# Strassen's seven block products in 8 of 32 pairs of k tiles of each down-projection sweep

## The chip, the cores and the metric

One NeuronCore of one Trainium2 chip runs the whole program in one launch. The metric is device time in microseconds (us). The kernel before took 2149.73, 2150.02 and 2151.38 us in three runs, median 2150.02 us.

## The reference

A two-layer encoder trunk on one sequence of 256 tokens, width 2048, all in float32. Each layer has an attention sub-layer (layer 0 differential attention, layer 1 windowed grouped-query attention with a sink, both with four memory heads) and an MLP. What matters here is the MLP:

```python
h = rms_norm(x, norm_mlp[i])
x = x + jnp.square(jax.nn.relu(h @ w_up[i])) @ w_down[i]
```

Per layer `w_up` is 2048 x 8192 and `w_down` 8192 x 2048, so the down projection multiplies 256 x 8192 by 8192 x 2048: 64 k tiles of 128 rows.

## The kernel before

**Splitting.** Every float32 operand of a large product is split into a part `hi` rounded to fp32r (ScalarE, a cast) and a rest `lo` (VectorE, `raw - hi`). A product is then three fp32r matmuls: hi x hi, hi x lo, lo x hi. Weights arrive as pieces of 128 x 1024 floats, 512 KB each. `fetch` (L171) issues the load on SyncE's queue into one of 4 `raw` buffers, and the split into one of 4 `hi` and 4 `lo` buffers. `piece` (L188) keeps two pieces ahead of the one in use; a list `plan` (L156 to L166) gives the order of all pieces.

**The MLP** (`mlp`, L647). The up projection leaves the hidden values feature-major in 16 tiles `hT`, the first six in the one large buffer `big` (which holds the attention bias table outside the MLP), the other ten in the pool `blk`. The down projection makes two sweeps per layer, one for each half of the 2048 output columns. A sweep holds four PSUM banks (`ps[n][t]`: two chunks of 512 columns by two tiles of 128 tokens; pool `mm` in the first sweep, `aux` in the second) and steps through 32 pairs of k tiles. A pair takes two weight pieces, one for each chunk, and two splits of hidden tiles (`h2_of`, into the pool `h2`), and issues 2 k tiles x 2 token tiles x 2 chunks x 3 = 24 matmuls of 128 x 128 by 128 x 512. A layer ends with `finish`, which adds the banks to the residual `xt`. In the last sweep of the program the last two pairs are held back, so that bank after bank can be finished and sent out.

**Order.** The engines run their instructions in order; a scheduler settles the order on each engine when the kernel is built, and can move a split ahead where its buffers are free. With 4 `hi` and 4 `lo` buffers, the split of the next pair starts when TensorE has ended the pair before the present one. The bias table of layer 1 is loaded back into `big` (`bias_load`, L579) in the second sweep of layer 0, once the hidden tiles in `big` have been read.

A pair's matmuls are these:

```python
for kk in range(2):
    for t in range(2):
        for n in range(2):
            mms(n, t, 2 * j + kk, *w2[n], x2[kk])
```

Of the kernel before, what the change touches and what calls it, by code (L numbers as in the profile page):

```python
# [14 lines left out]
F32 = mybir.dt.float32  # L15
# [4 lines left out]
ALU = mybir.AluOpType  # L20
# [14 lines left out]
WARM = 16  # L35
LAM_INIT = 0.8 - 0.6 * math.exp(-0.3 * 0)
# [10 lines left out]
def trunk(ctx: ExitStack, tc: tile.TileContext, xin, xtok, memin, pos, rel, gcol, rows,  # L47
# [19 lines left out]
    def half(tag):  # L67
        return xp.tile([P, 2, 256], F32R, tag=tag, name=nm(tag), bufs=16 if tag == "x2" else 12)

    def blk(shape, dt):  # L70
        return xp.tile(shape, dt, tag="blk", name=nm("blk"), bufs=10)
# [86 lines left out]
    def plan_down(name):  # L158
        plan.extend((name, c, j) for h in range(2) for j in range(32) for c in (2 * h, 2 * h + 1))
# [47 lines left out]
    def make_x2(src, g, tag="x2"):  # L207
        t = half(tag)
        split_gain(t[:, 0, :], t[:, 1, :], src, g)
        return t  # L210
# [161 lines left out]
    def diff_head(hl, qT, kT, v, bias, H2, hg):  # L372
# [62 lines left out]
        def finish():  # L435
# [9 lines left out]
    def plain_head(hl, kl, qT, kT, v, bias, sink, H2, hg, tag):  # L445
# [42 lines left out]
        def finish():  # L488
# [9 lines left out]
            t = half(tag)  # L498
            split(t[:, 0, :], t[:, 1, :], o)
            H2[hg] = t  # L500
# [106 lines left out]
    def mem_part(layer, qm, qd, H2):  # L607
        M2 = [None] * KT
        box = {}

        def before(j):
# [15 lines left out]
        heads = [plain_head(h, h, qm, kT, vbox, None, None, H2, 12 + h, "x2") for h in range(4)]  # L627
# [8 lines left out]
    def out_proj(layer, H2):  # L636
        X2 = [None] * KT
# [9 lines left out]
    def mlp(layer, X2, last):  # L647
        hT = []
        wide = big([P, 6, 4, S])
        for c in range(16):  # L650
# [3 lines left out]
            ht = wide[:, c] if c < 6 else blk([P, 4, S], F32)  # L654
# [6 lines left out]
        N2 = [None] * KT  # L661

        def h2_of(k):
            t = half("h2")
            split(t[:, 0, :], t[:, 1, :], hT[k // 4][:, k % 4, :])
            return t


        for half_ in range(2):
# [4 lines left out]
            def mms(n, t, k, hi, lo, x2):  # L674
                ws = slice((k % 2) * 512, (k % 2) * 512 + 512)
                xh = x2[:, 0, t * P:(t + 1) * P]
                xl = x2[:, 1, t * P:(t + 1) * P]
                nc.tensor.matmul(ps[n][t], lhsT=xh, rhs=hi[:, ws], start=(k == 0), stop=False)  # L678
                nc.tensor.matmul(ps[n][t], lhsT=xh, rhs=lo[:, ws], start=False, stop=False)  # L679
                nc.tensor.matmul(ps[n][t], lhsT=xl, rhs=hi[:, ws], start=False, stop=(k == 4 * KT - 1))  # L680

            def finish(n, t):
                c = chunks[n]
                d = xt[:, t, c * 512:(c + 1) * 512]
                nc.vector.scalar_tensor_tensor(d, ps[n][t], r2[:, t:t + 1], d, op0=ALU.mult, op1=ALU.add)
# [164 lines left out]
```

## Time and profile before

| quantity | value |
|---|---|
| median of 3 runs | 2150.02 us |
| the profiled execution's own time | 2150.42 us |
| its span | 2148.6 us |
| TensorE busy | 2137.6 us (99%) |
| VectorE busy | 1315.6 us (61%) |
| ScalarE busy | 1083.6 us (50%) |
| mean DMA rate | 190 GB/s |
| granted TensorE clock | 1.00 |

The span runs from the first to the last instruction; the execution's own time is 1.8 us longer. Busy shares are means over stages with different limits. A matmul's duration is longer than the distance to the next one, since matmuls are pipelined: the distance between starts is the pace. The four down sweeps begin at about 784.8, 958.9, 1795.0 and 1969.5 us.

### The profile page before, as it was taken

Reading aid. Unit: us, or ns where it says so; the run is one execution under the profiler, and the core shown is the slowest. Engines: PE = TensorE matmul, PEld = TensorE weight load, DVE = VectorE, ACT = ScalarE, POOL = GpSimd, SP = SyncE. Lnnn points to the kernel's source line nnn. Section 1 sums busy time; section 2 is a strip of 40 time slices with the busy share of each in tenths; the row PEclk is TensorE's granted clock in tenths of the full one; section 3 lists DMA queues with packets and bytes.
Section 4 is the critical chain, followed back from the end, with each engine's and each line's share of the span. In section 5 each row is a group of like instructions: output and inputs, shape, how many; then the busy total and the mean of one; then the engine's idle time right before and its main releaser. Section 6 shows DMA issues by size and latency. Waiting matters only on the chain.

```text
span 2148.6 us, 29416 instructions
## 1 busy us (share of the span) xinstructions
PE 2137.6 (99%) x11116; PEld 1806.4 (84%) x11116; DVE 1315.6 (61%) x2067; ACT 1083.6 (50%) x1740; POOL 35.7 (2%) x61
## 2 busy tenths in 40 slices
PE   9999999999999999999999999999999999999999
PEld 7877878888888888888888888888888888888887
DVE  7667786565555555566556677655555556556554
ACT  6456675454444445555545566554444444544443
POOL 1200020000000000000000000000000000000000
PEclk9999999999999999999999999999999999999999
DMA  8865565666666666666656656566666666666654
GB/s 292 237 209 154 157 195 153 187 183 189 185 194 188 191 186 193 193 195 235 198 194 192 181 167 178 155 183 183 185 195 188 192 189 185 196 196 212 192 193 148
DMA packets 114959, 409.24 MB, mean 190 GB/s; under 512 B 13568, under 2 KB 14336, under 8 KB 114560
## 3 DMA queue, kind: packets, MB, share of 16 engines
q1 hardware_dynamic: 111840, 401.01, 60.9%
q0 software_dynamic: 1536, 4.20, 0.8%
q10 hardware_dynamic: 1440, 2.15, 0.3%
q8 instruction: 87, 1.43, 0.3%
q14 instruction: 56, 0.46, 0.1%
HBM read 401.93 MB, written 5.37 MB: 190 GB/s over the span
## 4 chain that ended last, share of the span: by engine, by line
PE 97%; DMA 1%; DVE 1%; ACT 1%; issue 0%; SPq 0%; POOL 0%; ACTq 0%; DVEq 0%; POOLq 0%
PE mm L289 11%; PE aux L289 11%; PE mm L276 9%; PE mm L277 9%; PE mm L278 9%; PE mm L293 6%; PE aux L293 6%; PE mm L680 5%; PE mm L679 5%; PE mm L678 5%; PE aux L679 5%; PE aux L680 5%; PE aux L678 5%; DMA raw<-in_w_a 1%; PE aux L368 1%; PE aux L339 1%
## 5 line engine op out<-in xcount | busy, mean ns | idle before, releaser
L185 DVE TENSOR_TENSOR lo<-raw,hi 128x1024 fp32r<-128x1024 f32 (+1 forms) x744 | 892.7, 1214 | 747.7 <-ACT hi L184 747.3
L184 ACT CAST hi<-raw 128x1024 fp32r<-128x1024 f32 (+1 forms) x744 | 764.3, 1044 | 815.2 <-PE aux L289 194.1
L276 PE MATMUL mm<-hi,x 128*128 128x512 f32 x704 | 281.3, 401 | 2.0 <-ACT hi L184 2.0
L277 PE MATMUL mm<-lo,x 128*128 128x512 f32 x704 | 276.3, 392 | 2.1 <-DVE lo L185 2.1
L278 PE MATMUL mm<-hi,x 128*128 128x512 f32 x704 | 275.9, 392 | 0.0
L289 PE MATMUL mm<-x,hi 128*128 128x512 f32 x1024 | 247.4, 391 | 0.0
L289 PE MATMUL aux<-x,hi 128*128 128x512 f32 x1024 | 246.9, 391 | 0.0
L289 PEld LDWEIGHTS mm<-x,hi 128*128 128x128 f32 x1024 | 188.2, 188 | 36.8 <-DVE xt L642 0.5
L289 PEld LDWEIGHTS aux<-x,hi 128*128 128x128 f32 x1024 | 188.2, 188 | 36.4
L679 PE MATMUL aux<-lo,h 128*128 128x512 f32 x512 | 199.5, 390 | 0.5 <-DVE lo L185 0.5
L680 PE MATMUL aux<-hi,h 128*128 128x512 f32 x512 | 199.2, 389 | 0.0
L678 PE MATMUL aux<-hi,h 128*128 128x512 f32 x512 | 199.2, 389 | 0.0
L678 PE MATMUL mm<-hi,h 128*128 128x512 f32 x512 | 199.2, 389 | 0.0
L679 PE MATMUL mm<-lo,h 128*128 128x512 f32 x512 | 199.2, 389 | 0.0
L680 PE MATMUL mm<-hi,h 128*128 128x512 f32 x512 | 199.2, 389 | 0.0
L276 PEld LDWEIGHTS mm<-hi,x 128*128 128x128 f32 x704 | 132.2, 188 | 29.1 <-ACT hi L184 3.3
L277 PEld LDWEIGHTS mm<-lo,x 128*128 128x128 f32 x704 | 132.6, 188 | 28.2 <-DVE lo L185 4.2
L278 PEld LDWEIGHTS mm<-hi,x 128*128 128x128 f32 x704 | 132.2, 188 | 27.9 <-DVE x L201 0.2
L293 PEld LDWEIGHTS mm<-x,lo 128*128 128x128 f32 x1024 | 131.4, 191 | 4.8
L293 PEld LDWEIGHTS aux<-x,lo 128*128 128x128 f32 x1024 | 131.3, 191 | 5.0
L293 PE MATMUL mm<-x,lo 128*128 128x256 f32 x1024 | 133.3, 283 | 0.0
L293 PE MATMUL aux<-x,lo 128*128 128x256 f32 x1024 | 132.8, 283 | 0.0
(166 smaller groups left out, 2114.8 us busy)
## 6 DMA issues: line engine op xcount, KB each, us to landing
raw<-in_w_up SPq DMA_DIRECT2D x256, 512.0 KB, 3.9
raw<-in_w_down SPq DMA_DIRECT2D x256, 512.0 KB, 4.2
raw<-in_w_a SPq DMA_DIRECT2D x72, 512.0 KB, 4.0
raw<-in_w_out SPq DMA_DIRECT2D x64, 512.0 KB, 3.6
raw<-in_w_b SPq DMA_DIRECT2D x48, 512.0 KB, 3.7
raw<-in_w_mem SPq DMA_DIRECT2D x32, 512.0 KB, 3.8
raw<-in_w_a SPq DMA_DIRECT2D x16, 256.0 KB, 5.7
blk<-bkt POOLq DMA_DIRECT2D x32, 128.0 KB, 8.8
```

The costliest lines, as they stand in the source:

```text
L184: nc.scalar.copy(hi[:, s], raw[:, s])
L185: nc.vector.tensor_tensor(lo[:, s], raw[:, s], as32(hi)[:, s], op=ALU.subtract)
L276: nc.tensor.matmul(ps[t], lhsT=xh, rhs=hi[:, ws], start=(k == 0), stop=False)
L277: nc.tensor.matmul(ps[t], lhsT=xh, rhs=lo[:, ws], start=False, stop=False)
L278: nc.tensor.matmul(ps[t], lhsT=xl, rhs=hi[:, ws], start=False, stop=(k == KT - 1))
L289: nc.tensor.matmul(ps[o], lhsT=hi[:, cols(k % 2, o)], rhs=x2.rearrange("p a s -> p (a s)"), start=(k == 0), stop=(k == 2 * nj - 1))
L293: nc.tensor.matmul(ps[o][:, 256:512], lhsT=lo[:, cols(k % 2, o)], rhs=x2[:, 0, :], start=False, stop=False)
L339: nc.tensor.transpose(out=pt[:, h * P:(h + 1) * P], in_=qn[t][:, h * P:(h + 1) * P], identity=ident)
L368: nc.tensor.transpose(out=pt[:, kt * S + qt * P:kt * S + (qt + 1) * P], in_=p_of(qt)[:, kt * P:(kt + 1) * P], identity=ident)
L678: nc.tensor.matmul(ps[n][t], lhsT=xh, rhs=hi[:, ws], start=(k == 0), stop=False)
L679: nc.tensor.matmul(ps[n][t], lhsT=xh, rhs=lo[:, ws], start=False, stop=False)
L680: nc.tensor.matmul(ps[n][t], lhsT=xl, rhs=hi[:, ws], start=False, stop=(k == 4 * KT - 1))
```

## The change

In each sweep the pairs 5, 8, 11, 14, 17, 20, 23 and 26 (`FAST`) are computed as a 2 x 2 by 2 x 2 block product with seven block products instead of eight (the Winograd form of Strassen's scheme): the blocks are token tile by k tile on one side, k tile by column chunk on the other. Three of the products go straight into three of the four banks. The other four go into four more banks (`side`, the pool of the other sweep), summed over the eight fast pairs, and are added to the residual by `add_side` after pair 26.

- Weights are laid out anew on the host (`_pairs`): a piece now holds two of the four blocks of a pair, [b00, b11] and [b10, b01]. Bytes and number of pieces are the same. An ordinary pair's matmuls pick their block from either piece.
- `fetch_sums` makes for a fast pair two 128 x 1024 tiles of block sums of weights on VectorE and splits them like a piece; of the second piece only the first half is still split.
- `seven` makes four 128 x 128 block sums of the hidden tiles (`v`) and splits them.
- The pools `x2` and `h2` now hand out tiles of two k tiles (8 and 6 of them, before 16 and 12 halves), so one split covers 512 columns. The hidden tiles in `big` are now chunks 4 to 9, before 0 to 5. With that the load of the bias table stands in SyncE's queue behind the weight loads of pair 18 of the sweep, before behind those of pair 9.

```diff
+FAST = (5, 8, 11, 14, 17, 20, 23, 26)
...
     def plan_down(name):
-        plan.extend((name, c, j) for h in range(2) for j in range(32) for c in (2 * h, 2 * h + 1))
+        plan.extend((name, h, j) for h in range(2) for j in range(64))
...
+    def fetch_sums(key, raw, hi, lo):
+
+        first = newest[0]
+        tag = "blk" if key[:2] == ("down0", 1) else "x2"
+        a, b = quad(tag, (P, 2, 512), F32), quad(tag, (P, 2, 512), F32)
+        nc.vector.tensor_tensor(a, first.rearrange("p (a n) -> p a n", a=2),
+                                raw[:, 512:1024].unsqueeze(1).broadcast_to([P, 2, 512]), op=ALU.add)
+        nc.vector.tensor_tensor(b[:, 0, :], a[:, 1, :], first[:, 0:512], op=ALU.add)
+        nc.vector.tensor_tensor(b[:, 1, :], b[:, 0, :], raw[:, 0:512], op=ALU.add)
+        split(hi[:, 0:512], lo[:, 0:512], raw[:, 0:512])
+        ah, al, bh, bl = [quad("x2", (P, 2, 512)) for _ in range(4)]
+        split(ah, al, a)
+        split(bh, bl, b)
+        sums[key] = (ah, al, bh, bl)
...
+        seven = name.startswith("down") and j % 2 == 1 and j // 2 in FAST
...
             behind[0] = nc.sync.dma_start(raw[:, s], src[:, s])
-            nc.scalar.copy(hi[:, s], raw[:, s])
-            nc.vector.tensor_tensor(lo[:, s], raw[:, s], as32(hi)[:, s], op=ALU.subtract)
+            if seven:
+                fetch_sums((name, c, j), raw, hi, lo)
+            else:
+                split(hi[:, s], lo[:, s], raw[:, s])
...
-            ht = wide[:, c] if c < 6 else blk([P, 4, S], F32)
+            ht = wide[:, c - 4] if 4 <= c < 10 else blk([P, 4, S], F32)
...
+            def seven(j, two, x2):
+
+                ah, al, bh, bl = [v.rearrange("p a n -> p (a n)") for v in sums.pop((f"down{layer}", half_, 2 * j + 1))]
+                t2 = quad("h2", (P, 2, 512))
+                v = t2k([P, 512])
+                h = hidden(j)
+                h4 = h.rearrange("p (a s) -> p a s", a=4)
+                nc.vector.tensor_tensor(v[:, 0:256].rearrange("p (a s) -> p a s", a=2), h4[:, 0:4:3, :],
+                                        h4[:, 1:2, :].broadcast_to([P, 2, P]), op=ALU.subtract)
+                nc.vector.tensor_tensor(v[:, 256:384], h[:, 384:512], v[:, 0:128], op=ALU.add)
+                nc.vector.tensor_tensor(v[:, 384:512], h[:, 256:384], v[:, 256:384], op=ALU.subtract)
+                split(t2[:, 0, :], t2[:, 1, :], v)
+                at = [slice(i * P, (i + 1) * P) for i in range(4)]
+                f, e = j == FAST[0], j == FAST[-1]
+                three(side[0], f, e, x2, at[0], two[0], lower)
+                three(ps[0][0], False, False, x2, at[2], two[1], lower)
+                three(ps[1][0], False, False, t2, at[3], two[0], upper)
+                three(side[1], f, e, t2, at[0], (ah, al), upper)
+                three(side[3], f, e, t2, at[1], (ah, al), lower)
+                three(side[2], f, e, t2, at[2], (bh, bl), lower)
+                three(ps[0][1], False, False, x2, at[3], (bh, bl), upper)
...
+            def add_side():
+
+                q1, u2, u3, u4, u5 = [t2k([P, 512]) for _ in range(5)]
+                nc.scalar.copy(q1, side[0])
+                nc.vector.tensor_tensor(u2, side[2], q1, op=ALU.subtract)
+                nc.vector.tensor_tensor(u4, side[1], u2, op=ALU.subtract)
+                nc.vector.tensor_tensor(u3, u2, side[3], op=ALU.subtract)
+                nc.vector.tensor_tensor(u5, u3, side[1], op=ALU.subtract)
+                add_to(0, 0, q1)
+                add_to(0, 1, u4)
+                add_to(1, 0, u3)
+                add_to(1, 1, u5)
...
             for j in range(32):
-                w2 = [piece(f"down{layer}", c, j) for c in chunks]
-                x2 = [h2_of(2 * j), h2_of(2 * j + 1)]
+                if j == FAST[0]:
+                    side = [bank("aux" if half_ == 0 else "mm") for _ in range(4)]
+                two = [piece(f"down{layer}", half_, 2 * j + i) for i in range(2)]
+                x2 = h2_of(j)
...
+                if j in FAST:
+                    seven(j, two, x2)
+                else:
+                    for kk in range(2):
+                        for t in range(2):
+                            for n in range(2):
+                                mms(n, t, 2 * j + kk, two, x2)
+                if j == FAST[-1]:
+                    add_side()
```

`three` issues the three matmuls of a block product (hi x hi, hi x lo, lo x hi). The scheduler's order around a fast pair follows, at two places.

On VectorE before, in the first sweep of layer 0: the splits of pairs 10 (raw_8193, raw_8199), 11 (raw_8235, raw_8241) and 12, with two hidden tiles between.

```order
L185 TENSOR_TENSOR lo_8195<-raw_8193,hi_8194 128x1024
L185 TENSOR_TENSOR lo_8201<-raw_8199,hi_8200 128x1024
L205 TENSOR_TENSOR h_8418<-blk_6218,h_8418 128x256
L205 TENSOR_TENSOR h_8457<-blk_6218,h_8457 128x256
L185 TENSOR_TENSOR lo_8237<-raw_8235,hi_8236 128x1024
L185 TENSOR_TENSOR lo_8243<-raw_8241,hi_8242 128x1024
L205 TENSOR_TENSOR h_8460<-blk_6218,h_8460 128x256
L205 TENSOR_TENSOR h_8499<-blk_6415,h_8499 128x256
```

Now the same stretch: the splits of pair 10 (raw_8168, raw_8174), hidden tiles of pairs 12 and 13, the sums a (x_8217) and b (x_8218) of the fast pair 11 (raw_8207, raw_8213), their rests al and bl, the split of pair 11 itself, a hidden tile, and the split of pair 12.

```order
L242 TENSOR_TENSOR lo_8170<-raw_8168,hi_8169 128x1024
L242 TENSOR_TENSOR lo_8176<-raw_8174,hi_8175 128x1024
L242 TENSOR_TENSOR h_8314<-big_4604,h_8314 128x512
L242 TENSOR_TENSOR h_8366<-big_4604,h_8366 128x512
L194 TENSOR_TENSOR x_8217<-raw_8207,raw_8213 128x1024
L196 TENSOR_TENSOR x_8218<-x_8217,raw_8207 128x512
L197 TENSOR_TENSOR x_8218<-x_8218,raw_8213 128x512
L242 TENSOR_TENSOR x_8225<-x_8217,x_8224 128x1024
L242 TENSOR_TENSOR x_8227<-x_8218,x_8226 128x1024
L242 TENSOR_TENSOR lo_8209<-raw_8207,hi_8208 128x1024
L242 TENSOR_TENSOR lo_8215<-raw_8213,hi_8214 128x512
L242 TENSOR_TENSOR h_8405<-big_4604,h_8405 128x512
```

Between the splits of pairs 10 and 11 there were two operations of 256 columns; now there are two of 512, and the five of the sums, which stand ahead of the rests of pair 11 itself.

On TensorE, the last matmul of pair 10 and the start of pair 11, before (hi_8236 and hi_8242 are the two pieces) and now.

```order
L680 MATMUL mm_7814<-hi_8200,h_8250 128x512
L678 MATMUL mm_7811<-hi_8236,h_8289 128x512
L679 MATMUL mm_7811<-lo_8237,h_8289 128x512
L680 MATMUL mm_7811<-hi_8236,h_8289 128x512
L678 MATMUL mm_7813<-hi_8242,h_8289 128x512
L679 MATMUL mm_7813<-lo_8243,h_8289 128x512
```

```order
L713 MATMUL mm_7778<-hi_8169,h_8232 128x512
L711 MATMUL aux_7987<-hi_8208,h_8271 128x512
L712 MATMUL aux_7987<-lo_8209,h_8271 128x512
L713 MATMUL aux_7987<-hi_8208,h_8271 128x512
L711 MATMUL mm_7775<-hi_8214,h_8271 128x512
L712 MATMUL mm_7775<-lo_8215,h_8271 128x512
L713 MATMUL mm_7775<-hi_8214,h_8271 128x512
L711 MATMUL mm_7777<-hi_8208,h_8274 128x512
L712 MATMUL mm_7777<-lo_8209,h_8274 128x512
L713 MATMUL mm_7777<-hi_8208,h_8274 128x512
L711 MATMUL aux_7988<-x_8224,h_8274 128x512
```

The second matmul of the pair still needs the rest of the first piece, and the fifth that of the second piece; the sums (x_8224) are first read by the tenth. TensorE has 96 matmuls fewer in the whole program.

## Rows read from the trace of the kernel before

**Rows 1.** Page, part 1: engine, busy us, share of span, instructions.

```profile
PE 2137.6 (99%) x11116; PEld 1806.4 (84%) x11116; DVE 1315.6 (61%) x2067; ACT 1083.6 (50%) x1740; POOL 35.7 (2%) x61
```

**Rows 2.** Three sweeps: us, PE, PEld, DVE, ACT, POOL busy, clock, DMA, GB/s.

```profile
784.80:958.90 174.10, 174.10 (x770) 144.16 (x769) 103.29 (x138) 87.30 (x133) 0.00 (x0) 1.00 0.61 192
958.90:1134.00 175.10, 174.59 (x777) 144.13 (x776) 100.60 (x127) 87.71 (x131) 3.06 (x2) 1.00 0.64 207
...
1969.50:2144.50 175.00, 175.00 (x773) 144.63 (x771) 97.30 (x121) 81.01 (x115) 0.00 (x0) 1.00 0.58 189
```

**Rows 3.** TensorE's waits in layer 0's sweeps: us, times, longest.

```profile
PE aux L679 <- DVE lo L185: 0.5, 1, 0.5
```

**Rows 4.** TensorE, timeline, 72 matmuls in a row: start, duration, work.

```profile
859.83 0.39 PE L678 MATMUL mm<-hi,h 128*128 128x512 f32 x1
...
875.92 0.39 PE L680 MATMUL mm<-hi,h 128*128 128x512 f32 x1
```

**Rows 5.** VectorE, timeline, same stretch, one pair.

```profile
861.79 2.36 DVE L185 TENSOR_TENSOR lo<-raw,hi 128x1024 fp32r<-128x1024 f32 x2 [2.26 <-ACT hi L184]
864.07 0.90 DVE L205 TENSOR_TENSOR h<-blk,h 128x256 fp32r<-128x256 f32 x2
```

**Rows 6.** VectorE, groups by shape, whole span: busy us, mean ns, idle.

```profile
L185 DVE TENSOR_TENSOR lo<-raw,hi 128x1024 fp32r<-128x1024 f32 x728 | 881.7, 1225 | 747.5 <-ACT hi L184 747.3
...
L205 DVE TENSOR_TENSOR t2k<-aux,t2k 128x512 fp32r<-128x512 f32 x20 | 13.6, 684 | 0.0
...
L685 DVE SCALAR_TENSOR_TENSOR xt<-aux,r,xt 128x512 f32<-128x512 f32 x8 | 5.8, 751 | 6.7 <-PE aux L680 6.7
```

**Rows 7.** VectorE, timeline near the start; the last line needs the one before.

```profile
17.66 0.69 DVE L185 TENSOR_TENSOR lo<-raw,hi 128x512 fp32r<-128x512 f32 x1
18.26 0.16 DVE L597 TENSOR_TENSOR neglam<-sm 128x1 f32<-128x1 f32 x1
18.46 0.15 DVE L598 TENSOR_SCALAR neglam<-neglam 128x1 f32<-128x1 f32 x1
```

**Rows 8.** ScalarE, groups by shape, whole span.

```profile
L204 ACT CAST t2k<-aux 128x512 fp32r<-128x512 f32 x20 | 11.3, 583 | 0.0
```

**Rows 9.** TensorE, timeline of the last two pairs.

```profile
2132.95 0.39 PE L678 MATMUL aux<-hi,h 128*128 128x512 f32 x1
...
2134.99 0.61 PE L678 MATMUL aux<-hi,h 128*128 128x512 f32 x2
2135.52 0.50 PE L679 MATMUL aux<-lo,h 128*128 128x512 f32 x1
...
2136.32 0.40 PE L679 MATMUL aux<-lo,h 128*128 128x512 f32 x1
```

**Rows 10.** ScalarE, timeline, same stretch.

```profile
2133.15 2.01 ACT L184 CAST hi<-raw 128x1024 fp32r<-128x1024 f32 x2 [3.43 <-PE aux L680]
```

**Rows 11.** VectorE, timeline, same stretch.

```profile
2134.24 2.36 DVE L185 TENSOR_TENSOR lo<-raw,hi 128x1024 fp32r<-128x1024 f32 x2 [3.08 <-ACT hi L184]
```

**Rows 12.** SyncE's queue, a pair's first load issued.

```profile
863.05 0.33 SPq L183 DMA_DIRECT2D raw<-in_w_down  x1
```

**Rows 13.** Loads issued 863.6 to 865 (the pair's second): us to landing.

```profile
raw<-in_w_down SPq DMA_DIRECT2D x1, 512.0 KB, 4.5
```

**Rows 14.** Loads issued 862.8 to 863.6 (the first).

```profile
raw<-in_w_down SPq DMA_DIRECT2D x1, 512.0 KB, 3.6
```

**Rows 15.** SyncE's queue around the bias load.

```profile
996.92 0.42 SPq L581 DMA_DIRECT2D big<-bsv  x1
1000.85 1.46 SPq L183 DMA_DIRECT2D raw<-in_w_down  x2
```

**Rows 16.** The bias load: KB, us to landing.

```profile
big<-bsv SPq DMA_DIRECT2D x1, 3072.0 KB, 14.4
```

**Rows 17.** The two weight loads issued behind it.

```profile
raw<-in_w_down SPq DMA_DIRECT2D x2, 512.0 KB, 11.8
```

**Rows 18.** VectorE after the bias landed.

```profile
1013.79 1.83 DVE L185 TENSOR_TENSOR lo<-raw,hi 128x1024 fp32r<-128x1024 f32 x1 [2.85 <-ACT hi L184]
```

More of the change, by code (lines that the diff above doesn't have):

```diff
@@ L65, in bank, with quad, __init__, __getitem__ @@
         return pp.tile([P, 512], F32, tag=tag, name=nm(tag))
-    def half(tag):
-        return xp.tile([P, 2, 256], F32R, tag=tag, name=nm(tag), bufs=16 if tag == "x2" else 12)
+    def quad(tag, shape=(P, 2, 2, 256), dt=F32R):
+        return xp.tile(list(shape), dt, tag=tag, name=nm(tag), bufs={"x2": 8, "h2": 6, "blk": 10}[tag])
+    class Halves:
+        def __init__(self, tag_of=lambda pair: "x2"):
+            self.tag_of = tag_of
+            self.pairs = {}
+        def __getitem__(self, k):
+            return self.pairs[k // 2][:, k % 2]
+        def new(self, k):
+            if k // 2 not in self.pairs:
+                self.pairs[k // 2] = quad(self.tag_of(k // 2))
+            return self[k]
     def blk(shape, dt):
-        return xp.tile(shape, dt, tag="blk", name=nm("blk"), bufs=10)
+        return quad("blk", shape, dt)
     def big(shape):
@@ L205, in split, with make_x2 @@
         nc.vector.tensor_tensor(lo, src, as32(hi), op=ALU.subtract)
-    def make_x2(src, g, tag="x2"):
-        t = half(tag)
+    def make_x2(X2, k, src, g):
+        t = X2.new(k)
         split_gain(t[:, 0, :], t[:, 1, :], src, g)
-        return t
     def add_sq(k, src):
@@ L626, in mem_part @@
         vbox = [None, None]
-        heads = [plain_head(h, h, qm, kT, vbox, None, None, H2, 12 + h, "x2") for h in range(4)]
+        heads = [plain_head(h, h, qm, kT, vbox, None, None, H2, 12 + h) for h in range(4)]
         for h in heads:
@@ L660, in mlp, with hidden, h2_of @@
             hT.append(ht)
[L661 to L665, printed above, removed]
+        N2 = Halves()
+        def hidden(j):
+            return hT[j // 2].rearrange("p k s -> p (k s)")[:, (j % 2) * 512:(j % 2) * 512 + 512]
+        def h2_of(j):
+            t = quad("h2", (P, 2, 512))
+            split(t[:, 0, :], t[:, 1, :], hidden(j))
             return t
@@ L682, in finish, with three, mms @@
-            def finish(n, t):
+            def three(bank_, first_, last_, x2, xs, w2, ws):
+                nc.tensor.matmul(bank_, lhsT=x2[:, 0, xs], rhs=w2[0][:, ws], start=first_, stop=False)
+                nc.tensor.matmul(bank_, lhsT=x2[:, 0, xs], rhs=w2[1][:, ws], start=False, stop=False)
+                nc.tensor.matmul(bank_, lhsT=x2[:, 1, xs], rhs=w2[0][:, ws], start=False, stop=last_)
+            lower, upper = slice(0, 512), slice(512, 1024)
+            def mms(n, t, k, two, x2):
+                w2 = two[(k + n) % 2]
+                three(ps[n][t], k == 0, k == 4 * KT - 1, x2, slice((k % 2) * S + t * P, (k % 2) * S + (t + 1) * P), w2,
+                      upper if n else lower)
@@ L686, in finish @@
+            def finish(n, t):
+                c, d = add_to(n, t, ps[n][t])
                 if last:
@@ L703, in mlp @@
                 for t in range(2):
-                    for j, w2, x2 in held:
+                    for j, two, x2 in held:
                         for kk in range(2):
-                            mms(n, t, 2 * j + kk, *w2[n], x2[kk])
+                            mms(n, t, 2 * j + kk, two, x2)
                     finish(n, t)
```

60 lines of the change are left out of this document (29 added, 31 removed).

## The prediction

> **What bounds the kernel now.** The page's engine line comes first: TensorE is busy 99% of the span, VectorE 61%, ScalarE 50% [rows 1]. The table of the sweeps says the same of the place of the change, with the clock at full level and DMA at about 0.6 [rows 2]: TensorE never rests, and VectorE works 101 of 175 us. The waits confirm it: in both sweeps of layer 0 TensorE waited once, 0.5 us [rows 3]. Its timeline gives the pace: 71 steps from 859.83 to 875.92, so 0.2266 us per matmul [rows 4], and 24 of them make a pair of 5.44 us. So a matmul taken away is worth 0.2266 us, if nothing starts to wait.
>
> **The change part by part.**
>
> *Removed.* Three matmuls per fast pair, 8 fast pairs, 4 sweeps: 96 x 0.2266 = 21.75 us. A fast pair takes 21 x 0.2266 = 4.76 us, three pairs with one fast 15.64 instead of 16.32. The other operands have the old shapes, so the pace holds.
>
> *Added on VectorE.* Durations exceed the distance between starts: two rests of 1024 columns take 2.36 us together and one takes 1.225 [rows 5, 6], so the distance is 1.14; for 512 columns it is 0.60 to 0.61 [rows 7] at a duration of 0.68 [rows 6]. An operation that needs the result before it starts 0.04 after that one's end (18.46 after 18.26 + 0.16) [rows 7]. In three pairs with one fast stand eight operations of 1024 (five rests of pieces, a, al, bl) and seven of 512 (half a piece, two of b, three hidden tiles, t2): 9.1 + 4.3, with 0.2 for the two dependent starts of b and about 0.75 for the small sums `v` 14.4 us, beside 15.64 on TensorE. They fit, by 1.3 us. What counts is whether they come in time.
>
> *The chain of a fast pair F.* Zero is the first matmul of pair F-2. ScalarE's casts of F-1 wait for the end of F-3: in the last pairs TensorE starts a pair at 2132.95, the cast follows at 2133.15, the rests at 2134.24 and 1.14 later [rows 9 to 11], so 0.20, 1.27 and 2.41 here; two casts take 2.01, so 0.96 apart [rows 10]. Then, in the new order: two hidden tiles at 3.55 and 4.16 (their casts, 0.58 each [rows 8], are done by 3.3); a 4.77 to 5.99; the two halves of b, each dependent, 6.03 and 6.75, ending 7.43; al at 7.36 (its cast, 1.05 from 6.04, is done at 7.09); bl at 8.56, since its cast ends at 8.52; the rest of F's first piece 9.70 to 10.92; of the second, half as long, 10.84 to 11.53. TensorE starts F at 2 x 5.44 = 10.88, reads the first rest with its second matmul at 11.11 and the second with its fifth at 11.79. VectorE's end reaches TensorE 0.06 later (2134.24 + 1.22 against 2135.52) [rows 9, 11], so at 10.98 and 11.59. **The chain arrives 0.13 and 0.20 us early.** The sums themselves are read by the tenth matmul (12.9), with 2 us to spare. Then the split of F+1 waits for its buffers until 11.1 and ends at 14.5, before 15.87; VectorE rests about a microsecond before the next round. In this order stand pairs 11 to 26; before pairs 5 and 8 the pair's own rests stand ahead of bl, with over 1 us to spare. With one exception (the bias, below) that makes 23 tight pairs. What is queued behind the late casts of a and b is F's own cast on ScalarE, which ends at 9.5, before VectorE needs it.
>
> *The loads.* F's raw buffers are read until 10.92 and 11.53, so the loads of F+2 go out then. A pair's loads now land 3.6 us after the first issue (863.05) and about 5.6 after it for the second (issued 1.1 later, 4.5 to landing) [rows 12 to 14]: 14.5 and 16.6 here. The second cast of F+2 is due at 16.78: 0.2 us early again.
>
> So by the rows the steady stall is nothing, with 0.13 us in hand, against jitter of that size in loads and starts. Below nothing it can't go, since TensorE has no wait there to lose. Upward the bound is the full duration between starts (0.3, below) or more. I take 0.1 a pair: 23 x 0.1 = 2.3 us.
>
> By the Trainium skill, "VectorE: DVE Perf Modes", section "The DRAIN you can't avoid", the next VectorE operation does not start until the one before has left the pipeline. The trace agrees only for a dependent one: independent rests start 1.14 apart at a duration of 1.225 [rows 5, 6]. By the rule the stall would be that of the first rival and the time 2137.9 us, by the rows alone, without the 0.1 a pair, 2131.0 us.
>
> *add_side.* After pair 26: one copy on ScalarE, four VectorE operations of 512 (0.61) and four of 0.75 duration [rows 6], some 5.3 us a sweep. They read banks that TensorE ended with pair 26. With pair 26 at zero the rests of 28 run from 6.0 to 8.9 around the first of them, the burst ends near 12.8, and the rest of pair 29 at 14.5, needed at 15.87. TensorE covers it: nothing. Uncovered it would cost up to 4 x 5.3 = 21 us.
>
> *Start of the second sweep.* The small sums for six pairs are moved ahead into the first pairs. In layer 0 VectorE works at 957 to 977 on `finish`, splits and the next layer's inputs; its pauses take most of the 6 us, and by the same counting every rest stays ahead of its matmul. Nothing, up to 2 us.
>
> *The bias load.* It now goes out behind pair 18's loads, so while the chain of fast pair 17 runs, at about 4.9, instead of behind pair 9. It took 14.4 us [rows 15, 16], and the loads behind it, issued at 1000.85, landed 11.8 us later, 1.3 after it [rows 15, 17]. Here they land near 20.6 and 21.7; the rests of pair 19 then come at 23.0 and 24.1, against 21.3 and 22.0 needed. GpSimd's masking then slows one rest by 0.6 (1.83 instead of 1.22) [rows 18]. That is some 2.3 us less the 0.5 it costs today [rows 3]: I take 2, from 0 to 4. The sums of pair 20, which follow, are ordered around it.
>
> *The end.* In the held pairs the first bank now needs both pieces of each pair, not one. The last rest ends at 2135.38 + 1.22 = 2136.60; today the matmul at its place starts at 2136.32 [rows 9, 11]. 0.35 us.
>
> *Sum*, against the profiled execution's own 2150.42 us (span 2148.6 and 1.8 around it; 0.4 above the median of the runs, inside their spread): 2150.42 - 21.75 + 2.3 + 2 + 0.35 = **2133.3 us**.
>
> **Rivals.**
>
> 1. *VectorE's chain slips a little.* If each of the operations from the second rest of F-1 to the first rest of F took its full duration, the eight starts would be 0.07 to 0.08 later each where they are not already dependent: the rest of F's first piece reaches TensorE at 11.41 instead of 10.98, 0.30 late. Against it: the pairs of rests [rows 5]. For it: a margin of 0.13 on a chain of two engines that no row shows whole. 23 x 0.30 = 6.9 instead of 2.3: 2137.9 us; with slips of 0.6 a pair, 2145.
>
> 2. *Slower: the loop of the raw buffers becomes the bound.* F's buffers are freed late, the loads of F+2 start late, its split, the sums of F+3 and the split of F+3 follow, and TensorE waits once every three pairs. The loop has room for 5.3 us to the second landing. Each 0.1 us more costs 23 x 0.1 = 2.3 us; from 5.3 + (21.75 - 2.35) / 23 = 6.15 us the change loses. At 6.6 us: 2150.42 - 21.75 + 2.35 + 23 x 1.3 = 2161 us. For it: the two loads now go out 0.6 apart instead of 1.1, and landing reached 11.8 behind other traffic [rows 17]. Against it: 3.6 and 4.5 in the undisturbed sweep at a DMA share of 0.6 [rows 2, 13, 14].
>
> 3. *No wait at all appears* and the bias load is covered: 2150.42 - 21.75 + 0.35 = 2129.0 us.
>
> That the change does not do what it says is settled by the order: 96 matmuls fewer, the rest in the old sequence.
>
> **How the numbers follow.** Forecast (2130 to 2136) 0.50, rival 3 0.12, rival 1 from 2136 to 2145.7 0.23, slips between 2145.7 and 2154.3 0.07, rival 2 0.08. A measurement of this kernel tells 0.2%, 4.3 us, from no change: faster (under 2145.7) 0.85, same 0.07, slower 0.08. The range from 2128.5, a little under rival 3, to 2146 leaves out rival 2 and most of the slips that eat the gain; it holds about 0.84.
>
> **What would show it.** Right: TensorE's pace still 0.227; fast pairs of 4.76 us; in a first sweep TensorE's waits on VectorE's rests under 3 us in all, at the second or fifth matmul of pairs 11 to 26; sweeps near 169 us, the second of layer 0 some 2 us longer with a wait at pair 19; VectorE busy near 150 us a sweep. Rival 1: waits of 0.3 us or more at the second matmul of every fast pair, with VectorE without a pause from the rests of F-1 to those of F. Rival 2: ScalarE's second cast of F+2 waiting for its load, and VectorE idle behind it. Wrong altogether: waits of over 0.8 us per fast pair, or a matmul pace above 0.227 in the fast pairs.

## The result, and the profile after

Four runs of the changed kernel took 2126.74 to 2127.94 us, median **2127.34 us**; the kernel before, beside them, 2149.53 to 2151.38 us, median 2149.88 us. The ratio is 0.9894, 95% interval 0.9877 to 0.9911. The forecast was 2133.3 us with a range from 2128.5: the direction was right, the time lies 1.2 us below the range and 6.0 us below the forecast.

The page's engine line answers to [rows 1] (busy us, share, instructions): 96 matmuls fewer, and VectorE's share up from 61 to 70%.

```profile
PE 2116.4 (100%) x11020; PEld 1790.6 (84%) x11020; DVE 1497.5 (70%) x2259; ACT 1130.8 (53%) x1712; POOL 34.3 (2%) x61
```

The best view is the table of the four sweeps, cut at the first matmul of each (the second and the fourth end at the start of their last matmul). First the kernel before, cut likewise, which sharpens [rows 2]; then the changed one. Columns as there: window, length, then PE, PEld, DVE, ACT and POOL busy, clock, DMA, GB/s.

```profile
785.03:959.11 174.08, 174.08 (x770) 144.14 (x768) 103.27 (x138) 87.28 (x132) 0.00 (x0) 1.00 0.61 192
959.11:1135.82 176.71, 176.20 (x785) 145.46 (x783) 102.01 (x130) 88.32 (x134) 3.06 (x2) 1.00 0.64 208
1796.35:1970.43 174.08, 174.08 (x769) 144.14 (x768) 103.27 (x138) 86.79 (x130) 0.00 (x0) 1.00 0.62 192
1970.43:2144.50 174.07, 174.07 (x769) 143.88 (x767) 96.36 (x120) 80.53 (x115) 0.00 (x0) 1.00 0.57 188
```

```profile
785.33:953.97 168.64, 168.64 (x745) 139.69 (x744) 143.39 (x168) 98.98 (x125) 0.00 (x0) 1.00 0.58 198
953.97:1124.18 170.21, 170.21 (x760) 141.16 (x759) 148.40 (x184) 101.61 (x133) 3.50 (x2) 1.00 0.63 216
1784.72:1953.36 168.64, 168.64 (x745) 139.64 (x744) 147.54 (x186) 98.35 (x123) 0.00 (x0) 1.00 0.60 199
1953.36:2122.02 168.66, 168.66 (x744) 139.34 (x743) 137.82 (x156) 93.49 (x114) 0.00 (x0) 1.00 0.58 194
```

The first and third sweep are shorter by 5.44 us each, which is 24 x 0.2266 to the last digit: no fast pair waits. The second is shorter by 6.50: 5.44, and the 1.06 us that TensorE lost at the bias load of before (e_big, below). The last is shorter by 5.41, so the end costs 0.03. Ahead of the first sweep 0.30 us more is spent. -5.44 x 2 - 6.50 - 5.41 + 0.30 = -22.49, and the spans differ by 22.5 (2148.6 to 2126.1).

TensorE's waits in the whole span (us, times, longest) lie outside the sweeps, at lines of the first stretch and of attention; the wait of [rows 3] has no successor:

```profile
PE mm L313 <- DVE lo L242: 2.6, 1, 2.6
PE aux L115 <- DVE tab L572: 1.1, 1, 1.1
PE aux L404 <- DVE t2k L443: 1.1, 1, 1.1
...
```

A fast pair (11), the start of pair 12 and the first matmuls of the next fast pair (14), from TensorE's timeline: 843.81 to 848.57 is 4.76 us, 21 matmuls at the old pace of [rows 4].

```profile
843.81 0.39 PE L711 MATMUL aux<-hi,h 128*128 128x512 f32 x1
...
848.57 0.39 PE L711 MATMUL mm<-hi,h 128*128 128x512 f32 x1
...
859.45 0.39 PE L711 MATMUL aux<-hi,h 128*128 128x512 f32 x1
859.68 0.39 PE L712 MATMUL aux<-lo,h 128*128 128x512 f32 x1
```

The chain of F = 14, which the prediction counted from the start of pair F-2 = 12 (848.57 here), on ScalarE and then on VectorE:

```profile
846.59 1.05 ACT L241 CAST hi<-raw 128x1024 fp32r<-128x1024 f32 x1 [0.70 <-DMA raw<-in_w_down]
847.82 1.05 ACT L241 CAST hi<-raw 128x1024 fp32r<-128x1024 f32 x1 [0.17 <-DMA raw<-in_w_down]
```

```profile
847.68 2.45 DVE L242 TENSOR_TENSOR lo<-raw,hi 128x1024 fp32r<-128x1024 f32 x2 [0.26 <-ACT hi L241]
850.05 1.29 DVE L242 TENSOR_TENSOR h<-big,h 128x512 fp32r<-128x512 f32 x2
851.34 1.23 DVE L194 TENSOR_TENSOR x<-raw,raw 128x1024 f32<-128x1024 f32 x1
852.60 0.69 DVE L196 TENSOR_TENSOR x<-x,raw 128x512 f32<-128x512 f32 x1
853.32 0.69 DVE L197 TENSOR_TENSOR x<-x,raw 128x512 f32<-128x512 f32 x1
853.93 2.42 DVE L242 TENSOR_TENSOR x<-x,x 128x1024 fp32r<-128x1024 f32 x2
856.27 1.82 DVE L242 TENSOR_TENSOR lo<-raw,hi 128x1024 fp32r<-128x1024 f32 x2
```

Every step stands in the order that was counted, at nearly the distances that were counted, but 1.9 to 2.2 us earlier: the casts at -1.98 and -0.75 (counted 0.20 and 1.16), a at 2.77 (4.77), the rest of F's first piece at 7.70 (9.70). That rest ends at 857.49, reaches TensorE at 857.55 (with the 0.06 us of the prediction), and is read at 859.68: **2.13 us in hand, where the prediction had 0.13.** Over the 32 fast pairs this margin is 0.69 to 3.10 us, median 2.04.

The casts of pair 13 waited for their loads, no longer for TensorE. The same trace shows what differs. The buffers of pair 13's splits are given back by the fast pair 11; those of pair 15's by the plain pair 13, and its casts start 0.44 us before the first matmul of pair 14 (859.45):

```profile
859.01 2.00 ACT L241 CAST hi<-raw 128x1024 fp32r<-128x1024 f32 x2 [1.93 <-issue]
```

Counted from the first matmul after the pair that gives the buffers back, the first cast stands at -0.44 us in 26 of 28 places behind a plain pair, and at -1.32 to -2.77 in 27 of 28 behind a fast one; the other one is at the bias load. In 21 of these 28 the sum a then waits for a load of F, 0.3 to 2.5 us: with the buffers free, the load is the next limit.

### The profile page after: what moved, and what is told of

The parts are those of the page before. It is cut to its first block, busy times and chain, and to the rows that moved or that the text cites. A ratio compares the mean times of both kernels' runs of the same rounds, so it can differ in the third digit from the quotient of the medians.

```text
span 2126.1 us, 29324 instructions
## 1 busy us (share of the span) xinstructions
PE 2116.4 (100%) x11020; PEld 1790.6 (84%) x11020; DVE 1497.5 (70%) x2259; ACT 1130.8 (53%) x1712; POOL 34.3 (2%) x61
## 4 chain that ended last, share of the span: by engine, by line
PE 97%; DMA 1%; DVE 1%; ACT 1%; issue 0%; SPq 0%; POOL 0%; ACTq 0%; DVEq 0%; POOLq 0%
PE mm L325 11%; PE aux L325 11%; PE mm L312 9%; PE mm L314 9%; PE mm L313 9%; PE mm L329 6%; PE aux L329 6%; PE aux L711 5%; PE aux L712 5%; PE mm L711 5%; PE mm L712 5%; PE aux L713 5%; PE mm L713 5%; PE aux L404 1%; DMA raw<-in_w_a 1%; PE aux L375 1%
## 5 line engine op out<-in xcount | busy, mean ns | idle before, releaser
L242 DVE TENSOR_TENSOR lo<-raw,hi 128x1024 fp32r<-128x1024 f32 (+1 forms) x744 | 875.4, 1190 | 535.3 <-ACT hi L241 534.0
L241 ACT CAST hi<-raw 128x1024 fp32r<-128x1024 f32 (+1 forms) x744 | 751.7, 1024 | 760.9 <-PE aux L325 193.5
L712 PE MATMUL aux<-lo,h 128*128 128x512 f32 x432 | 168.2, 389 | 0.0
L713 PE MATMUL aux<-hi,h 128*128 128x512 f32 x432 | 168.1, 389 | 0.0
L711 PE MATMUL aux<-hi,h 128*128 128x512 f32 x432 | 168.1, 389 | 0.0
L711 PE MATMUL mm<-hi,h 128*128 128x512 f32 x432 | 168.0, 389 | 0.0
L712 PE MATMUL mm<-lo,h 128*128 128x512 f32 x432 | 168.0, 389 | 0.0
L713 PE MATMUL mm<-hi,h 128*128 128x512 f32 x432 | 168.0, 389 | 0.0
```

The costliest lines, as they stand in the source:

```text
L241: nc.scalar.copy(hi, src)
L242: nc.vector.tensor_tensor(lo, src, as32(hi), op=ALU.subtract)
L711: nc.tensor.matmul(bank_, lhsT=x2[:, 0, xs], rhs=w2[0][:, ws], start=first_, stop=False)
L712: nc.tensor.matmul(bank_, lhsT=x2[:, 0, xs], rhs=w2[1][:, ws], start=False, stop=False)
L713: nc.tensor.matmul(bank_, lhsT=x2[:, 1, xs], rhs=w2[0][:, ws], start=False, stop=last_)
```

## Experiments

Each sweep's length, cut as above, is the sharpest measure; the stretch ahead of the first sweep, which no kernel here changes on purpose, ran from 782.8 to 787.1 us over the profiled runs and blurs the times. The ratio is to the kernel before on the same chip.

| kernel | median us | ratio (95%) | sweep 1 | 2 | 3 | 4 |
|---|---|---|---|---|---|---|
| before (profile shown) | 2149.88 | 1 | 174.08 | 176.71 | 174.08 | 174.07 |
| changed | 2127.34 | 0.9894 (0.9877-0.9911) | 168.64 | 170.21 | 168.64 | 168.66 |
| changed, again | 2127.59 | 0.9900 (0.9886-0.9914) | 168.64 | 170.21 | 168.64 | 168.64 |
| e_big | 2149.37 | 0.9998 (0.9989-1.0007) | 174.08 | 175.65 | 174.08 | 174.06 |
| e_plain | 2149.12 | 1.0000 (0.9991-1.0009) | 174.08 | 175.65 | 174.08 | 174.07 |
| e_dve | 2128.97 | 0.9903 (0.9888-0.9918) | 168.64 | 170.95 | 168.64 | 169.07 |
| e_dve2 | 2150.18 | 1.0006 (0.9996-1.0015) | 174.62 | 177.50 | 172.96 | 174.25 |
| e_late | 2128.94 | 0.9905 (0.9891-0.9918) | 168.64 | 170.37 | 168.66 | 168.64 |
| e_late_dve | 2137.62 | 0.9941 (0.9927-0.9954) | 169.56 | 172.43 | 169.65 | 172.30 |
| e_hold | 2131.13 | 0.9915 (0.9902-0.9929) | 168.64 | 173.39 | 168.66 | 168.63 |
| e_hold_dve | 2146.31 | 0.9987 (0.9978-0.9996) | 172.52 | 174.11 | 172.59 | 174.60 |
| e_ten | 2121.96 | 0.9873 (0.9858-0.9888) | 167.28 | 169.53 | 167.28 | 168.67 |
| e_best | 2122.92 | 0.9879 (0.9865-0.9892) | 167.28 | 169.57 | 167.28 | 167.79 |
| e_dense | 2129.32 | 0.9903 (0.9886-0.9919) | 165.92 | 172.59 | 166.88 | 171.53 |

**The bias load alone (e_big)**, and **everything but the fast pairs (e_plain)**.

```diff
 e_big, in the kernel before
-            ht = wide[:, c] if c < 6 else blk([P, 4, S], F32)
+            ht = wide[:, c - 4] if 4 <= c < 10 else blk([P, 4, S], F32)
 e_plain, in the changed kernel
-FAST = (5, 8, 11, 14, 17, 20, 23, 26)
+FAST = ()
...
```

> The kernel before with one edit: the bias load of layer 1 gets its buffers later, so it goes out where the changed kernel sends it (behind the loads of pair 18 instead of pair 9). Theory (the bias load's move is a gain): the four gaps of TensorE at 1015 to 1017 us, 1.06 us in all, go and none comes near pair 19: 2149.9 - 1.1 = 2148.8 us. Rival (the prediction's step): the rests of pair 19 come up to 2 us late: 2149.9 + 2 = 2151.9 us, with a wait at pair 19. With no fast pair in front of it pair 19 could have more cover than in the changed kernel; so a gain here supports the theory, and only a wait at pair 19 would support the rival.

> The changed kernel with an empty list of fast pairs: its new weight layout, buffers in quads, order of the last pairs and the place of the bias load stay, and every pair has 24 matmuls. Theory (the fast pairs give exactly their 96 matmuls, and what else the change does is worth 1.06 from the bias load, +0.3 at the start and +0.03 at the end): 2127.3 + 21.76 = 2149.1 us. Rival (the fast pairs cost a hidden stall of about 2.3 us that something else in the change gives back): 2127.3 + 21.76 - 2.3 = 2146.8 us.

The second sweep of e_big, columns as above:

```profile
959.22:1134.88 175.66, 175.66 (x785) 145.66 (x784) 102.55 (x130) 88.52 (x134) 3.24 (x2) 1.00 0.63 209
```

In both the second sweep takes 175.65 us, 1.06 less than before, and no wait of TensorE is listed in it; the other sweeps are unchanged. The times, 2149.37 and 2149.12 us beside 2149.43, cannot tell 1.06 us; the sweeps can. So the theory stands and the rival (+2, with a wait) falls. From e_plain to the changed kernel the sweeps lose 5.44, 5.44, 5.44 and 5.41 us: the fast pairs give their 96 matmuls whole. The bias load still costs cover: in e_big the rests of pair 18 are 1.85 and 0.74 us early instead of 3.77 and 3.32.

**How much does VectorE have in hand? (e_dve, e_dve2)** One or two useless sums per fast pair, between the splits of a and b:

```diff
         split(ah, al, a)
+        nc.vector.tensor_tensor(bl, a, b, op=ALU.add)
         split(bh, bl, b)
```

> The changed kernel with one useless VectorE sum of 128 x 1024 more in each fast pair, ahead of the rest of bl: 1.14 us from start to start, on the chain that the prediction called 0.13 us early. Theory (about 2.1 us are in hand): it is absorbed; VectorE then works some 15.5 of the 15.64 us of three pairs; 2127.3 to 2129 us. Rival (the prediction's margin of 0.13): 23 x 1.0 = 23 us more, 2150 us.

> The changed kernel with two such sums more in each fast pair. Theory (it is now VectorE's total that counts, 14.4 + 2 x 1.14 = 16.7 us against 15.64 on TensorE): some 1.0 us for each fast pair once the 2.1 us in hand are used up, so 27 to 30 x 1.0: about 2155 us, with VectorE without a pause and TensorE waiting on VectorE's rests in every fast pair. Rival (the prediction's frame, chain 0.13 early): 23 x 2.15 = 49 us more, 2177 us. If VectorE's total is smaller than counted: under 2145 us.

One sum more per fast pair, 1.14 us, cost 1.15 us in all four sweeps together. This does not measure the chain, though. On VectorE the sum (L201) took the place of bl, and bl went behind F's rests, as here for F = 14 of the first sweep, after al:

```profile
855.09 1.22 DVE L201 TENSOR_TENSOR x<-x,x 128x1024 fp32r<-128x1024 f32 x1
856.23 1.82 DVE L243 TENSOR_TENSOR lo<-raw,hi 128x1024 fp32r<-128x1024 f32 x2
857.97 1.22 DVE L243 TENSOR_TENSOR x<-x,x 128x1024 fp32r<-128x1024 f32 x1
```

So as many operations as before stand ahead of F's rest, and its margin is 2.08 us, beside 2.13. What refutes the 0.13 is the changed kernel's own trace, above; e_dve shows that VectorE's total has room for the 1.14 but for short waits in the second and the last sweep (0.74 and 0.41 us). Two sums cost 23.2 us, 0.72 per fast pair and the whole gain (about 2155 us was expected, 2150.18 measured). TensorE's waits in the first sweep of e_dve2 are now on VectorE's split of the sums:

```profile
PE aux L714 <- DVE x L244: 3.8, 6, 1.0
```

They recur at the same place of pair 8 and of every third pair; the matmul ahead of the first and of the seventh starts here, on TensorE's timeline:

```profile
830.96 0.39 PE L713 MATMUL aux<-x,h 128*128 128x512 f32 x1
...
929.61 0.39 PE L713 MATMUL aux<-x,h 128*128 128x512 f32 x1
```

So three pairs take 98.65 / 6 = 16.44 us. VectorE sets that nearly alone: in the 18 pairs from pair 9 of the first sweep on it is busy 94.70 of 98.51 us, and its pauses are for loads. These 18 pairs in e_dve2, then in the changed kernel, columns as above:

```profile
833.63:932.14 98.51, 95.70 (x416) 77.24 (x414) 94.70 (x105) 59.22 (x75) 0.00 (x0) 1.00 0.58 192
832.93:926.77 93.84, 93.84 (x415) 77.73 (x414) 82.66 (x91) 58.80 (x74) 0.00 (x0) 1.00 0.59 203
```

In the changed kernel VectorE works 82.66 / 6 = 13.8 us for three pairs with one fast; e_dve2 gives 94.70 / 6 - 2 x 1.14 = 13.5. The prediction had counted 14.4, with 0.75 for the small sums `v`; none of those stands in these 18 pairs.

**Where do the two microseconds come from? (e_late, e_late_dve, e_hold, e_hold_dve)** In the changed kernel a fast pair reads its own two pieces in its first three products only, so their buffers come free early in the pair. e_late puts the product that reads piece one last. e_hold also keeps the second piece's `hi` to the end. The arithmetic is the same. In both, the products that read the sums move up: bl is read by the 14th matmul of the pair in e_late and by the 13th in e_hold, where the changed kernel reads it with the 17th.

```diff
 e_late
                 three(ps[0][0], False, False, x2, at[2], two[1], lower)
-                three(ps[1][0], False, False, t2, at[3], two[0], upper)
...
                 three(ps[0][1], False, False, x2, at[3], (bh, bl), upper)
+                three(ps[1][0], False, False, t2, at[3], two[0], upper)
 e_hold, in addition
-                three(ps[0][0], False, False, x2, at[2], two[1], lower)
+                nc.tensor.matmul(ps[0][0], lhsT=x2[:, 0, at[2]], rhs=two[1][0][:, lower], start=False, stop=False)
+                nc.tensor.matmul(ps[0][0], lhsT=x2[:, 0, at[2]], rhs=two[1][1][:, lower], start=False, stop=False)
...
                 three(ps[0][1], False, False, x2, at[3], (bh, bl), upper)
+                nc.tensor.matmul(ps[0][0], lhsT=x2[:, 1, at[2]], rhs=two[1][0][:, lower], start=False, stop=False)
                 three(ps[1][0], False, False, t2, at[3], two[0], upper)
```

e_late_dve and e_hold_dve have the useless sum of e_dve besides.

> The changed kernel, but in a fast pair the product that reads the first piece alone stands last of the seven, so the buffers of the fast pair's first piece come free at the end of the pair, some 2 us later. Theory (the slack of the chain comes from a fast pair's pieces being read for the last time early in it): the chain of VectorE falls back to about the 0.13 us that the prediction had, the rest of the first piece of the next fast pair ends less than 0.6 us ahead of its matmul instead of about 2.1, and the time is between 2127.3 and 2131 us. Rival (the chain is early for another reason, loads or shorter operations): the rest still ends some 2 us ahead, and the time is 2127.3 us.

> As the run before it, with one useless VectorE sum of 128 x 1024 more in each fast pair, ahead of the rest of bl (1.14 us from start to start). Theory (early release gave the slack, and without it at most 0.13 to 0.6 us is left): each of some 23 to 27 tight fast pairs stalls 0.5 to 1.0 us: 2127.3 + 12 to 27 = 2139 to 2154 us. Rival (the slack of 2 us is there for another reason): it is absorbed, 2127.3 to 2129 us.

> The changed kernel, but in a fast pair the product of the first piece and the last matmul of the product that reads the second piece stand at the end, so that the hi buffers of both pieces stay in use to the end of the pair, as in a plain pair; the first rests are needed at the same matmuls as before. The run that held one piece only let the split of one piece go early. Theory (the early release of both pieces is what puts the chain 2 us ahead): the sum a starts about 4.2 to 4.8 us after the start of pair F-2 instead of 2.8, and the rest of F's first piece is done 0.1 to 0.8 us before its matmul, instead of about 2; no regular stall: 2127 to 2129.5 us. Rival (the loads or a shorter chain put it ahead): a still starts 2.8 us after, the margin stays near 2, 2127.3 us.

> As the run before it, with one useless VectorE sum of 128 x 1024 more per fast pair (1.14 us from start to start), which the changed kernel took at a cost of 1 us in all. Theory (only 0.1 to 0.8 us are left when the buffers are held): 0.35 to 1.0 us are lost in each of some 23 to 27 fast pairs, so 8 to 27 us: 2135 to 2154 us. Rival (margin still near 2): 2127.3 to 2129 us.

e_late missed: its time is inside the bounds, but the margin at pair 14 is 2.78 us, not under 0.6. One piece alone still went early (cast at 845.71; the other at 848.68, where pair 12 starts at 848.48), and the order on VectorE changed: a now stands ahead of the second hidden tile, bl behind F's rests. e_late_dve lost 7.8 us in its sweeps, short of the 12 to 27 expected.

e_hold does hold both. The start of pair 12, ScalarE's casts of 13 and VectorE's chain:

```profile
846.64 0.39 PE L711 MATMUL mm<-hi,h 128*128 128x512 f32 x1
```

```profile
846.16 2.01 ACT L241 CAST hi<-raw 128x1024 fp32r<-128x1024 f32 x2 [2.20 <-PE mm L743]
```

```profile
847.25 2.36 DVE L242 TENSOR_TENSOR lo<-raw,hi 128x1024 fp32r<-128x1024 f32 x2 [1.76 <-ACT hi L241]
849.60 1.23 DVE L194 TENSOR_TENSOR x<-raw,raw 128x1024 f32<-128x1024 f32 x1
...
854.28 1.82 DVE L242 TENSOR_TENSOR lo<-raw,hi 128x1024 fp32r<-128x1024 f32 x2
856.02 1.22 DVE L242 TENSOR_TENSOR x<-x,x 128x1024 fp32r<-128x1024 f32 x1
```

The casts now wait for TensorE, at -0.48 and +0.48 us from the pair's start instead of -1.98 and -0.75. Yet a comes at 2.96, not at 4.2 to 4.8, and the first rest of 14 is 2.19 us early: the order changed with the buffers, and bl (856.02) took the late place. The expectation's margin missed: e_hold shows that the release sets the casts, but not what late release costs in the order of the changed kernel; a kernel with late release in that order was not tried. Three sweeps cost nothing; the second costs 3.18 us, at the bias load, which goes out at 1042.15 there, 9.4 us after pair 15 starts (3.0 in the changed kernel), and at pairs 20 and 28.

e_hold_dve lost 17.7 us in the four sweeps (e_hold alone 3.2), inside the 8 to 27 expected, where e_dve lost 1.15. This is not the price of the release alone, since two more things differ. bl is needed four matmuls sooner, 4 x 0.2266 = 0.91 us, and on VectorE the useless sum and bl both stand behind F's rests. F's first rest itself was never late there (0.13 us early or more). Away from the bias load, all waits inside fast pairs are for bl, up to 0.9 us; the rest of the loss is at the rests of plain pairs behind them, pair 28 above all. So the time was hit by another way than the one expected. Here are the wait in the middle of pair 17 of the third sweep, and that pair's sum a, which had waited 1.76 us for a load:

```profile
1886.34 0.39 PE L712 MATMUL aux<-x,h 128*128 128x512 f32 x1
1887.13 0.50 PE L713 MATMUL aux<-x,h 128*128 128x512 f32 x1 [0.40 <-DVE x L243]
```

```profile
1877.69 1.23 DVE L194 TENSOR_TENSOR x<-raw,raw 128x1024 f32<-128x1024 f32 x1 [1.76 <-DMA raw<-in_w_down]
```

**More fast pairs (e_ten, e_best, e_dense).** The list is made to depend on the sweep (`B` for the first sweep of a layer, `A` for the second; in e_ten and e_dense also `B` for the very last).

```diff
-FAST = (5, 8, 11, 14, 17, 20, 23, 26)
 e_ten, e_best
+FAST_A = (5, 8, 11, 14, 17, 20, 23, 26, 29)
+FAST_B = (2, 5, 8, 11, 14, 17, 20, 23, 26, 29)
 e_dense
+FAST_A = (5, 7, 10, 12, 15, 17, 20, 22, 25, 27)
+FAST_B = (2, 4, 7, 9, 12, 14, 17, 19, 22, 24, 27, 29)
```

> The changed kernel with fast pairs every third pair from 2 to 29 in three sweeps and from 5 to 29 in the second sweep of layer 0: 39 fast pairs instead of 32. Theory (each fast pair is worth 3 x 0.2266 = 0.68 us and nothing waits): 2127.3 - 7 x 0.68 = 2122.6 us. Rival (the first and the last pairs of a sweep have no cover: sums for pair 2 fall into the work at a sweep's start, those of add_side into its end): up to 3 us of waits in a sweep, 2123 to 2134 us.

> The changed kernel with fast pairs two in every five (12 of 32 pairs in three sweeps, 10 in the second sweep of layer 0): 46 instead of 32. Theory (a fast pair adds some 5.3 us to VectorE, and five pairs with two fast need 2.5 x as much as TensorE has, VectorE 12.9 against TensorE 12.9 us for each 2.5 pairs): the gain of 14 x 0.68 = 9.5 us comes nearly whole if the order leaves no pauses, 2118 us, and is eaten where it does: 2118 to 2135 us, with VectorE over 95% busy in the sweeps. Rival (the prediction's frame): a fast pair two pairs after another has its chain shorter by a pair: over 1 us for each of some 20 such pairs, over 2138 us.

> Fast pairs every third pair from 2 to 29 in the first sweep of each layer, and from 5 to 29 in the second: 38 instead of 32. In the run with 39 the three sweeps but the last gained the whole 0.68 us per fast pair, and the last lost 1.3 us in two waits at pairs 14 and 20. Theory (the sums for pair 2 of the last sweep, made while the banks of the sweep before are finished, put VectorE behind): without them the waits go, so 2127.3 - 6 x 0.68 = 2123.2 us against the changed kernel beside it. Rival (the waits come from late loads, not from pair 2): they stay, 2124.5 us.

> The changed kernel itself once more, beside the three that follow, so that they are compared on the same chip. Expected: within 1 us of 2127.3 us, and the sweeps of the down projection as long as before (337.3 us for the two of layer 1); only the stretch ahead of the first sweep may differ by a microsecond or two, since the first loads set it.

e_best beats both kernels: 2122.92 us beside 2127.59 of the changed kernel on the same chip. Its sweeps are 1.36, 0.64, 1.36 and 0.85 us shorter, 4.2 for 18 matmuls (4.1), without a wait in any. e_ten gained its price in three sweeps and nothing in the last, where its margins at pairs 14 and 20 were -0.01; with pair 2 left out there e_best has 1.71 and 1.10. That fits the theory, on one profile each: a repeat of the changed kernel gave the same sweeps and 2127.59 us, but its margin at pair 8 of the last sweep was 2.96 us, beside 1.03. The times of e_ten and e_best cannot be told apart.

e_dense has 42 matmuls fewer than the changed kernel and no gain (its sweeps are 0.8 us longer together). Its first and last sweep:

```profile
785.91:951.83 165.92, 165.92 (x733) 137.39 (x732) 160.60 (x199) 107.45 (x137) 0.00 (x0) 1.00 0.60 201
1951.85:2123.38 171.53, 168.72 (x733) 136.27 (x731) 164.01 (x215) 102.88 (x128) 0.00 (x0) 1.00 0.58 195
```

VectorE is busy 160.6 of 165.9 us in the first, which still gains 2.72 (4 x 0.68); the others wait. The expectation's count, 12.9 against 12.9 us, puts the break-even near there. But of the 5.4 us that TensorE waits in the last sweep, 3.2 are at pairs 2 to 4, so the total in the steady part is not the whole cause, and the other sweeps were not followed further.

## Why the prediction was too slow, step by step

- *Removed, -21.75:* right. Measured -21.76 with the end's 0.03 taken out; pace 0.2266 and 4.76 us per fast pair.
- *The steady stall, +2.3:* measured 0. **The step that failed is "ScalarE's casts of F-1 wait for the end of F-3", with the 0.20 us behind it.** At F = 14 the first of them started 1.98 us before that end. Two errors lie in the step. The 0.20 was read at the last two pairs of the program [rows 9, 10], which run in the held order. In the middle of a sweep of the kernel before, the casts start ahead of the pair, not at its start as the text on the order had it, because a pair's last three matmuls read one of its two pieces only, and the other's buffer is free 0.68 us sooner:

```profile
861.19 0.39 PE L678 MATMUL mm<-hi,h 128*128 128x512 f32 x1
```

```profile
860.71 2.01 ACT L184 CAST hi<-raw 128x1024 fp32r<-128x1024 f32 x2 [1.63 <-PE mm L680]
```

  That is -0.48, and e_hold shows the same -0.48: 0.68 us, which [rows 5] already held (a rest at 861.79, 0.60 after the pair's start, against the 1.27 counted; [rows 9, 11] give 1.29). Corrected for this error alone the chain would have been 0.81 early, and the stall already nothing. The rest, about 1.3 us, is the fast pair's early release: F-3 is itself a fast pair, and its pieces are done with after three of its seven products. That the release sets the casts is shown by e_hold, and by the casts behind plain and fast pairs in the changed kernel. What this is worth in the margin is an estimate: at pair 14 VectorE runs from the second rest of 13 to the rest of 14 without a pause but the 0.03 us ahead of each dependent sum, so with the second cast at 0.48 instead of -0.75 the 2.13 us would have been 0.90. No run has late release in this order.
- *The distances on VectorE:* right. Two independent rests lie 1.14 apart at 1.22, and dependent ones start 0.03 after the end before (852.60 after 851.34 + 1.23). The paragraph that the prediction set beside the first rival (the Trainium skill, "VectorE: DVE Perf Modes", section "The DRAIN you can't avoid") goes on to say that a next operation which is not held starts earlier, and the independent ones here do.
- *The bias load, +2:* measured -1.06, and this is the largest miss, 3.06 us. The load of before did cost TensorE 1.06 us in gaps at 1015 to 1017, twice the 0.5 that the waits named [rows 3]. What was to replace it did not come, because the load rides on the same chain. SyncE's queue, and the landing times (KB, us) of the bias load and of the two loads behind it:

```profile
1037.66 0.33 SPq L614 DMA_DIRECT2D big<-bsv  x1
1043.77 0.93 SPq L217 DMA_DIRECT2D raw<-in_w_down  x2
```

```profile
big<-bsv SPq DMA_DIRECT2D x1, 3072.0 KB, 12.2
```

```profile
raw<-in_w_down SPq DMA_DIRECT2D x2, 512.0 KB, 7.7
```

  It went out 3.0 us after pair 15's start (1034.65), not 4.9; the loads behind it landed 7.7 us after their issue, not 11.8 [rows 17]. The rests of pair 19 start at 1053.94 and 1055.07, 19.3 and 20.4 us after pair 15's start, where 23.0 and 24.1 were counted, and are 0.75 and 0.29 us early:

```profile
1053.94 2.35 DVE L242 TENSOR_TENSOR lo<-raw,hi 128x1024 fp32r<-128x1024 f32 x2
```

  So the cover was used up almost whole; e_hold, with the load later, pays. Why the bias load lands after 12.2 us behind pair 18 (in e_big too) and after 14.4 in the old place stays open.
- *The end, +0.35:* measured 0.03. Which matmul reads the last rest was counted from the order of today's pairs; it was not followed further.
- *add_side and the start of the second sweep, 0:* right; no wait there. *VectorE's total, 14.4 us:* 0.6 too large; 13.8 measured, and `v` falls outside the steady part.
- *The base:* the sum started from the profiled execution, 2150.42 us, and the median before is 2149.88; this is 0.5 of the 6.0 us.
- *The range:* its low end, 2128.5, lay a little under the third rival, 2129.0 us, which set the bias load to nothing. A cost that goes was not allowed to be a gain. The 1.06 us, the 0.32 at the end and the 0.54 of the base, less the 0.30 ahead of the first sweep, lead from 2129.0 to 2127.4.

## What to carry over

Read the release of a buffer from the steady part of the loop and from the new order of reads: which product reads the tile last decides when its refill starts, and that can give the next stage microseconds that the changed work then uses. When one engine's work is traded for another's, count the second engine's total per period and its margin at the deadline separately; here one fast pair in three left no wait, and two in five did so in one sweep of four. An operation that is added to probe a margin may change the order, and with it what is probed: read where it landed. A load that is moved needs both prices, the one it stops costing and the one it will cost, and both depend on when its chain lets it go.

## Unexpected on the chip

GpSimd's masking of the landed bias table slowed VectorE more than in [rows 18]: two hidden-tile operations of 128x512, 0.69 us elsewhere, took 3.54 together (1.60 and 2.03).

```profile
1049.97 1.55 POOL L616 TENSOR_SCALAR_AFFINE_SELECT big<-big 128x1536 f32<-128x1536 f32 x1 [744.21 <-DMA big<-bsv]
1051.47 2.00 POOL L618 TENSOR_SCALAR_AFFINE_SELECT big<-big 128x1536 f32<-128x1536 f32 x1
```

```profile
1050.47 3.54 DVE L242 TENSOR_TENSOR h<-blk,h 128x512 fp32r<-128x512 f32 x2 [1.32 <-ACT h L241]
```

The Trainium skill, "SBUF — State Buffer", section "SBUF: two separate sides", says that GpSimd and a VectorE operation with two SBUF inputs take a shared port in turn, each for its whole instruction. The trace agrees: each of the two ends about 0.55 us after the GpSimd instruction that it overlaps (1052.07 after 1051.52, 1054.01 after 1053.47), nearly its own length. So what VectorE lost here went by the length of GpSimd's instruction, not by that of its own.
